# Grouped instance norm in units of 32 channels instead of 16: two 4 MB halves per unit, statistics summed in PSUM

## The chip, the cores and the metric

The kernel runs on one core of a Trainium2 chip. The metric is device time in microseconds (us), one figure per execution; lower is better. The profile is one execution taken by the hardware profiler, with times in us from the start of its span.

With one core there is no second die to compare, so a run is called slow only when it is more than 1.5% above the fastest run of the same kernel.

## The reference

The input is a float32 tensor of 4 x 8 x 16 x 256 x 256, which is 512 channels of 65536 elements, 134 MB. Each channel is normalized by its own mean and variance and scaled by a factor:

```python
mu = x.mean(axis=(3, 4), keepdims=True)
var = ((x - mu) ** 2).mean(axis=(3, 4), keepdims=True)
out = (x - mu) / np.sqrt(var + 1e-5) * gamma[None, :, :, None, None]
```

134 MB must be read and 134 MB written. The arithmetic per element is small.

## The kernel before

A unit is 16 channels. Each channel lies on 8 partitions, so a unit is one tile of 128 partitions x 8192 float32, 4 MB, contiguous in memory. There are 32 units and six tile buffers. SyncE issues the loads, ScalarE the stores. A load into a buffer waits for the store that last used it.

```python
S = 8; K = P // S; F = HW // S; U = n_ch // K      # 16 channels, 8192 columns, 32 units
data = tc.tile_pool(name="data", bufs=6)
for u in range(6): load(u)                         # nc.sync.dma_start, 4 MB each
...
for u in range(U):
    # statistics: one VectorE sum, two ScalarE squares with accumulated sums
    nc.vector.reduce_sum(out=sums[:, 0:1], in_=t[:], axis=AX.X)
    for c in range(0, F, 4096):
        nc.scalar.activation(out=junk[:], in_=t[:, c:c+4096], func=Square, accum_out=sqs[:, n:n+1])
    # ... matmul with a block matrix sums the 8 partitions of a channel;
    # ... eight small VectorE operations and one Sqrt make scale and shift
    # normalization, split: 5376 columns on VectorE, 2816 on ScalarE
    nc.vector.tensor_scalar(out=t[:, :5376], in0=t[:, :5376], scalar1=scale, scalar2=shift, ...)
    nc.scalar.activation(out=t[:, 5376:], in_=t[:, 5376:], func=Identity, bias=shift, scale=scale)
    nc.scalar.dma_start(out=ov[u], in_=t[:])       # the store, 4 MB
    if u + 6 < U: load(u + 6)
```

## Time and profile before

The median was 628.86 us of three runs (628.77 to 629.19) when the prediction was made.

| What | Value | Where it is read |
|---|---|---|
| DMA engines busy | 0.9 or more in all slices but the first and last | the page, slices |
| Bytes moved | 427 to 435 GB/s in most slices | the page, slices |
| VectorE, ScalarE busy | 66%, 54% of the span | the page, part 1 |
| Waits for loads | VectorE 150.4 us, ScalarE 163.5 us | the waits |

These lines are from the page of the kernel before. The lines DMA and GB/s cut the span into 40 slices; each digit is the busy share of the 16 DMA engines in tenths. The queue lines give packets, megabytes and share of all 16 DMA engines (q1 is loads, q10 stores). The line that starts with L109 is a group of instructions, the sums: shapes and count, then busy time and the mean ns of one, then the idle time ahead of them and what ended it. The last two are transfers, with the median time from issue to landing at the end.

```profile
span 627.1 us, 937 instructions
...
PE 22.3 (4%) x80; PEld 19.5 (3%) x80; DVE 416.5 (66%) x324; ACT 336.9 (54%) x194; POOL 1.2 (0%) x7
...
DMA  8999999999999999999999999999999999999997
GB/s 368 435 403 433 435 435 435 433 435 435 435 433 435 435 435 431 433 428 433 435 427 435 431 435 433 433 433 435 435 433 435 435 435 435 433 433 435 435 433 314
...
q1 hardware_dynamic: 4608, 134.22, 49.9%
q10 hardware_dynamic: 4610, 134.22, 49.6%
...
DVE 67%; another core or an unknown queue 23%; PE 3%; DMA 2%; ACT 2%; issue 1%
...
L109 DVE TENSOR_REDUCE sums<-xt 128x1 f32<-128x8192 f32 x32 | 277.9, 8686 | 150.4 <-DMA xt<-in_x_dram 150.4
...
xt<-in_x_dram SPq DMA_DIRECT2D x32, 4096.0 KB, 60.4
out_dram<-xt ACTq DMA_DIRECT2D x32, 4096.0 KB, 41.3
```

The waits of the kernel before, in us in total, count and longest:

```profile
ACT junk L111 <- DMA xt<-in_x_dram: 163.5, 29, 10.4
DVE sums L109 <- DMA xt<-in_x_dram: 150.4, 29, 6.5
```

The DMA engines are full from end to end: 49.9% of their time goes to loads and 49.6% to stores. VectorE and ScalarE wait for loads. The chain names VectorE for 67%, but it walks back along whatever came last; the waits show that the reductions themselves wait for data.

The columns of the timeline are start, duration, engine, line, operation.

```profile
24.30 3.08 DVE L147 TENSOR_SCALAR xt<-xt,scale,shift 128x5376 f32<-128x5376 f32 x1
24.36 2.73 ACT L153 ACTIVATE xt<-xt,shift,scale 128x2816 f32<-128x2816 f32 x1 [0.68 <-DVE shift L143]
...
27.46 0.38 ACTq L168 DMA_DIRECT2D out_dram<-xt  x1
```

```profile
598.43 8.69 DVE L109 TENSOR_REDUCE sums<-xt 128x1 f32<-128x8192 f32 x1 [5.13 <-DMA xt<-in_x_dram]
...
612.76 0.34 ACTq L168 DMA_DIRECT2D out_dram<-xt  x1
```

The first store is issued at 27.46 us, when VectorE has ended its part of the normalization. The last reduction starts at 598.43 us, when the last tile has landed.

### The profile page before, as it was taken

To read this page: it belongs to the slowest core of one execution; us is meant where nothing else is said; L and a number is where in the kernel's file an instruction comes from. 1 tells how busy PE (TensorE), PEld (TensorE's weight loads), DVE (VectorE), ACT (ScalarE), POOL (GpSimd) and SP (SyncE) were. 2 spreads that over 40 slices of the span, in tenths; PEclk is the share of its full clock that TensorE was granted. 3 is DMA by queue.
4 is the path that set the end of the run, shared out by engine and by line. 5 is a ranking of instruction groups with operands and counts; after the bars stand their busy time and mean duration, and the time that the engine had idled before them with its cause. 6 is when DMAs were issued, how large, how long until landed. Compare 5 with 4: busy or idle time off the path is not lost.

```text
span 627.1 us, 937 instructions
## 1 busy us (share of the span) xinstructions
PE 22.3 (4%) x80; PEld 19.5 (3%) x80; DVE 416.5 (66%) x324; ACT 336.9 (54%) x194; POOL 1.2 (0%) x7
## 2 busy tenths in 40 slices
PE   2000000000000000000000000000000000000000
PEld 2000000000000000000000000000000000000000
DVE  2999657766577665686656866558665577655770
ACT  2877536555456464464634646446554455544560
POOL 0000000000000000000000000000000000000000
DMA  8999999999999999999999999999999999999997
GB/s 368 435 403 433 435 435 435 433 435 435 435 433 435 435 435 431 433 428 433 435 427 435 431 435 433 433 433 435 435 433 435 435 435 435 433 433 435 435 433 314
DMA packets 9224, 268.49 MB, mean 428 GB/s; under 512 B 1025, under 2 KB 1026, under 8 KB 1026
## 3 DMA queue, kind: packets, MB, share of 16 engines
q1 hardware_dynamic: 4608, 134.22, 49.9%
q10 hardware_dynamic: 4610, 134.22, 49.6%
q14 instruction: 6, 0.05, 0.0%
HBM read 134.22 MB, written 134.22 MB: 428 GB/s over the span
## 4 chain that ended last, share of the span: by engine, by line
DVE 67%; another core or an unknown queue 23%; PE 3%; DMA 2%; ACT 2%; issue 1%
DVE sums L109 44%; DVE xt L147 16%; PE ps L120 3%; DMA xt<-in_x_dram 2%; ACT std L136 2%; DVE var L131 1%; DVE rstd L138 1%; DVE cm L125 1%; DVE shift L143 1%; DVE scale L141 1%; DVE nmean L127 1%; DVE mv L117 1%; DVE mv L118 0%
## 5 line engine op out<-in xcount | busy, mean ns | idle before, releaser
L109 DVE TENSOR_REDUCE sums<-xt 128x1 f32<-128x8192 f32 x32 | 277.9, 8686 | 150.4 <-DMA xt<-in_x_dram 150.4
L111 ACT ACTIVATE junk<-xt 128x4096 bf16<-128x4096 f32 x64 | 231.5, 3617 | 166.8 <-DMA xt<-in_x_dram 163.5
L147 DVE TENSOR_SCALAR xt<-xt,scale,shift 128x5376 f32<-128x5376 f32 x32 | 98.5, 3079 | 1.2
L153 ACT ACTIVATE xt<-xt,shift,scale 128x2816 f32<-128x2816 f32 x32 | 87.5, 2734 | 22.0 <-DVE shift L143 22.0
L136 ACT ACTIVATE std<-var,eps_t 128x1 f32<-128x1 f32 x32 | 9.4, 294 | 85.4 <-DVE var L131 85.4
L120 PE MATMUL ps<-mv,avg 128*128 128x2 f32 x64 | 18.7, 362 | 582.9 <-DVE mv L118 582.9
L120 PEld LDWEIGHTS ps<-mv,avg 128*128 128x128 f32 x64 | 16.0, 311 | 585.6 <-DVE mv L118 569.8
L125 DVE COPY cm<-ps 128x2 f32<-128x2 f32 x32 | 5.1, 160 | 21.8 <-PE ps L120 21.8
L138 DVE RECIPROCAL rstd<-std 128x1 f32<-128x1 f32 x32 | 5.2, 164 | 11.6 <-ACT std L136 11.6
L111 ACT ACTIVATION_READ_ACCUMULATOR junk<-xt 128x1 f32 x64 | 11.9, 186 | 0.0
L131 DVE SCALAR_TENSOR_TENSOR var<-cm,nmean 128x1 f32<-128x1 f32 x32 | 7.0, 220 | 1.1
L143 DVE TENSOR_TENSOR shift<-nmean,scale 128x1 f32<-128x1 f32 x32 | 5.1, 159 | 1.1
L141 DVE TENSOR_TENSOR scale<-rstd,g_col 128x1 f32<-128x1 f32 x32 | 5.1, 159 | 1.1
L117 DVE TENSOR_REDUCE mv<-sums 128x1 f32<-128x1 f32 x32 | 4.9, 154 | 1.1
L127 DVE TENSOR_SCALAR nmean<-cm 128x1 f32<-128x1 f32 x32 | 4.9, 153 | 1.1
L118 DVE TENSOR_REDUCE mv<-sqs 128x1 f32<-128x2 f32 x32 | 4.7, 145 | 0.0
L92 PE MATMUL g_ps<-one,g_rep 1*128 1x1 f32 x16 | 3.6, 348 | 2.8 <-DVE g_rep L86 2.8
L92 PEld LDWEIGHTS g_ps<-one,g_rep 1*128 1x128 f32 x16 | 3.5, 325 | 2.8 <-DVE g_rep L86 2.8
L99 DVE COPY g_col<-g_ps 128x8 f32<-128x8 f32 x1 | 0.2, 167 | 3.7 <-PE g_ps L92 3.7
L111 ACT ACT_TABLE_LOAD x1 | 1.3, 1283 | 1.4 <-PEq L185 1.4
L86 DVE COPY g_rep<-g_row 1x1024 f32<-1x1024 f32 x1 | 0.7, 681 | 1.1 <-DMA g_row<-in_gamma_dram 1.1
L136 ACT ACT_TABLE_LOAD x1 | 1.3, 1283 | 0.0
(9 smaller groups left out, 1.5 us busy)
## 6 DMA issues: line engine op xcount, KB each, us to landing
xt<-in_x_dram SPq DMA_DIRECT2D x32, 4096.0 KB, 60.4
out_dram<-xt ACTq DMA_DIRECT2D x32, 4096.0 KB, 41.3
g_row<-in_gamma_dram ACTq DMA_DIRECT2D x1, 0.5 KB
```

What stands on the lines that cost most here:

```text
L109: nc.vector.reduce_sum(out=sums[:, j : j + 1], in_=t[:, a:b], axis=AX.X)
L111: nc.scalar.activation(out=junk[:], in_=t[:, c : c + SQ], func=ACTF.Square, accum_out=sqs[:, n : n + 1],)
L117: nc.vector.reduce_sum(out=mv[:, 0:1], in_=sums[:], axis=AX.X)
L120: nc.tensor.matmul(out=ps[:], lhsT=avg[:].rearrange("p k s -> p (k s)"), rhs=mv[:], start=True, stop=True,)
L125: nc.vector.tensor_copy(out=cm[:], in_=ps[:])
L131: nc.vector.scalar_tensor_tensor(out=var[:], in0=cm[:, 0:1], scalar=nmean[:], in1=cm[:, 1:2], op0=ALU.mult, op1=ALU.add,)
L136: nc.scalar.activation(out=std[:], in_=var[:], func=ACTF.Sqrt, bias=eps_t[:], scale=1.0)
L138: nc.vector.reciprocal(out=rstd[:], in_=std[:])
L141: nc.vector.tensor_mul(out=scale[:], in0=rstd[:], in1=g_col[:, g : g + 1])
L143: nc.vector.tensor_mul(out=shift[:], in0=nmean[:], in1=scale[:])
L147: nc.vector.tensor_scalar(out=t[:, a:b], in0=t[:, a:b], scalar1=scale[:], scalar2=shift[:], op0=ALU.mult, op1=ALU.add,)
L153: nc.scalar.activation(out=t[:, a:b], in_=t[:, a:b], func=ACTF.Identity, bias=shift[:], scale=scale[:],)
```

## The change

The intent is fewer instructions. A unit becomes 32 channels on 4 partitions each, 128 partitions x 16384 float32, moved as two 4 MB halves. The partial sums of both halves are accumulated in PSUM by two matmuls, so that one short chain of small operations serves 32 channels. The square of a half is one instruction that writes bytes. The first half is normalized by VectorE alone and the second by ScalarE alone.

```diff
-    S = 8
+    S = 4
+    CW = F // 2
+    AHEAD = 3
-    data = ctx.enter_context(tc.tile_pool(name="data", bufs=6))
+    data = ctx.enter_context(tc.tile_pool(name="data", bufs=2 * AHEAD))
     def load(u):
+        for h in range(2):
+            t = data.tile([P, CW], F32, name="xt")
+            nc.sync.dma_start(out=t[:], in_=xv[u, :, h * CW : (h + 1) * CW])
+            tiles[u, h] = t
...
+        for h in range(2):
+            t = tiles[u, h]
+            nc.vector.reduce_sum(out=st[:, 2 * h : 2 * h + 1], in_=t[:], axis=AX.X)
+            nc.scalar.activation(out=junk[:], in_=t[:], func=ACTF.Square,
+                                 accum_out=st[:, 2 * h + 1 : 2 * h + 2])     # junk is uint8
+            nc.tensor.matmul(out=ps[:], lhsT=navg_w, rhs=st[:, 2 * h : 2 * h + 2],
+                             start=h == 0, stop=h == 1)
...                                       # nvar from PSUM, Sqrt, reciprocal, scale, shift
-            norm_vector(t, 0, DV, scale, shift)
-            norm_scalar(t, DV, F, scale, shift)
-            nc.scalar.dma_start(out=ov[u], in_=t[:])
-        if u + 6 < U:
-            load(u + 6)
+        nc.vector.tensor_scalar(out=ta[:], in0=ta[:], scalar1=scale, scalar2=shift, ...)
+        nc.scalar.activation(out=tb[:], in_=tb[:], func=ACTF.Identity, bias=shift, scale=scale)
+        nc.scalar.dma_start(out=ov[u, :, 0:CW], in_=ta[:])
+        nc.scalar.dma_start(out=ov[u, :, CW:F], in_=tb[:])
+        if u + AHEAD < U:
+            load(u + AHEAD)
```

In memory, a half is now 128 rows of 32 KB at a pitch of 64 KB. Before, a tile was 128 rows of 32 KB that followed each other.

More of the change, by code (lines that the diff above doesn't have):

```diff
@@ L27 @@
     n_ch = B * G * C
-    S = 8
+    S = 4
     K = P // S
     F = HW // S
+    CW = F // 2
     U = n_ch // K
     NG = (G * C) // K
-    SQ = 4096
-    DV = 5376
-    assert HW % S == 0 and (G * C) % K == 0 and F % SQ == 0
+    AHEAD = 3
+    assert HW % S == 0 and (G * C) % K == 0
     xv = x.rearrange("b g c h w -> (b g c h w)").rearrange("(u p f) -> u p f", p=P, f=F)
@@ L45 @@
     ctx.enter_context(tc.manual_schedule())
-    def spans(widths):
-        edges = [0]
-        for w in widths:
-            edges.append(edges[-1] + w)
-        assert edges[-1] == F
-        return list(zip(edges[:-1], edges[1:]))
-    load_spans, store_spans = {}, {}
-    whole = spans([F])
     tiles = {}
     def load(u):
-        t = data.tile([P, F], F32, name="xt")
-        for a, b in load_spans.get(u, whole):
-            nc.sync.dma_start(out=t[:, a:b], in_=xv[u, :, a:b])
-        tiles[u] = t
-    for u in range(6):
+        for h in range(2):
+            t = data.tile([P, CW], F32, name="xt")
+            nc.sync.dma_start(out=t[:], in_=xv[u, :, h * CW : (h + 1) * CW])
+            tiles[u, h] = t
+    for u in range(AHEAD):
         load(u)
@@ L71 @@
     eps_t = singles.tile([P, 1], F32, name="eps_t")
-    nc.vector.memset(eps_t[:], 1e-5)
-    avg = singles.tile([P, K, S], F32, name="avg")
-    nc.gpsimd.memset(avg[:], 1.0 / HW)
+    nc.gpsimd.memset(eps_t[:], 1e-5)
+    one = singles.tile([1, 1], F32, name="one")
+    nc.gpsimd.memset(one[:], 1.0)
+    navg = singles.tile([P, K, S], F32, name="navg")
+    nc.gpsimd.memset(navg[:], -1.0 / HW)
     nc.gpsimd.affine_select(
-        out=avg[:], in_=avg[:], pattern=[[-S, K], [0, S]], compare_op=ALU.is_ge,
+        out=navg[:], in_=navg[:], pattern=[[-S, K], [0, S]], compare_op=ALU.is_ge,
         fill=0.0, base=0, channel_multiplier=1,
@@ L79 @@
     nc.gpsimd.affine_select(
-        out=avg[:], in_=avg[:], pattern=[[S, K], [0, S]], compare_op=ALU.is_ge,
+        out=navg[:], in_=navg[:], pattern=[[S, K], [0, S]], compare_op=ALU.is_ge,
         fill=0.0, base=S - 1, channel_multiplier=-1,
     )
-    one = singles.tile([1, 1], F32, name="one")
-    nc.vector.memset(one[:], 1.0)
+    navg_w = navg[:].rearrange("p k s -> p (k s)")
     g_rep = singles.tile([1, NG, K, S], F32, name="g_rep")
@@ L99 @@
     nc.vector.tensor_copy(out=g_col[:], in_=g_ps[:])
-    junk = singles.tile([P, SQ], BF16, name="junk")
-    def coefficients(u):
-        t = tiles[u]
-        sums = stats_pool.tile([P, len(load_spans.get(u, whole))], F32, name="sums")
-        sqs = stats_pool.tile([P, F // SQ], F32, name="sqs")
-        n = 0
-        for j, (a, b) in enumerate(load_spans.get(u, whole)):
-            nc.vector.reduce_sum(out=sums[:, j : j + 1], in_=t[:, a:b], axis=AX.X)
-            for c in range(a, b, SQ):
-                nc.scalar.activation(
-                    out=junk[:], in_=t[:, c : c + SQ], func=ACTF.Square,
-                    accum_out=sqs[:, n : n + 1],
-                )
-                n += 1
-        mv = stats_pool.tile([P, 2], F32, name="mv")
-        nc.vector.reduce_sum(out=mv[:, 0:1], in_=sums[:], axis=AX.X)
-        nc.vector.reduce_sum(out=mv[:, 1:2], in_=sqs[:], axis=AX.X)
-        ps = psum.tile([P, 2], F32, name="ps")
-        nc.tensor.matmul(
-            out=ps[:], lhsT=avg[:].rearrange("p k s -> p (k s)"), rhs=mv[:],
-            start=True, stop=True,
-        )
-        cm = stats_pool.tile([P, 2], F32, name="cm")
-        nc.vector.tensor_copy(out=cm[:], in_=ps[:])
-        nmean = stats_pool.tile([P, 1], F32, name="nmean")
-        nc.vector.tensor_scalar(
-            out=nmean[:], in0=cm[:, 0:1], scalar1=-1.0, scalar2=None, op0=ALU.mult,
-        )
-        var = stats_pool.tile([P, 1], F32, name="var")
-        nc.vector.scalar_tensor_tensor(
-            out=var[:], in0=cm[:, 0:1], scalar=nmean[:], in1=cm[:, 1:2],
@@ new lines @@
+    junk = singles.tile([P, CW], mybir.dt.uint8, name="junk")
+    for u in range(U):
+        st = stats_pool.tile([P, 4], F32, name="st")
+        ps = psum.tile([P, 2], F32, name="ps")
+        for h in range(2):
+            t = tiles[u, h]
+            nc.vector.reduce_sum(out=st[:, 2 * h : 2 * h + 1], in_=t[:], axis=AX.X)
+            nc.scalar.activation(
+                out=junk[:], in_=t[:], func=ACTF.Square,
+                accum_out=st[:, 2 * h + 1 : 2 * h + 2],
+            )
+            nc.tensor.matmul(
+                out=ps[:], lhsT=navg_w, rhs=st[:, 2 * h : 2 * h + 2],
+                start=h == 0, stop=h == 1,
+            )
+        nmean = ps[:, 0:1]
+        nvar = stats_pool.tile([P, 1], F32, name="nvar")
+        nc.vector.tensor_scalar(
+            out=nvar[:], in0=nmean, scalar1=nmean, scalar2=ps[:, 1:2],
@@ L135, in coefficients @@
         std = stats_pool.tile([P, 1], F32, name="std")
-        nc.scalar.activation(out=std[:], in_=var[:], func=ACTF.Sqrt, bias=eps_t[:], scale=1.0)
-        rstd = stats_pool.tile([P, 1], F32, name="rstd")
-        nc.vector.reciprocal(out=rstd[:], in_=std[:])
-        scale = stats_pool.tile([P, 1], F32, name="scale")
-        g = u % NG
-        nc.vector.tensor_mul(out=scale[:], in0=rstd[:], in1=g_col[:, g : g + 1])
-        shift = stats_pool.tile([P, 1], F32, name="shift")
-        nc.vector.tensor_mul(out=shift[:], in0=nmean[:], in1=scale[:])
@@ L144, in coefficients @@
-        return scale, shift
-    def norm_vector(t, a, b, scale, shift):
+        nc.scalar.activation(out=std[:], in_=nvar[:], func=ACTF.Sqrt, bias=eps_t[:], scale=-1.0)
+        coef = stats_pool.tile([P, 2], F32, name="coef")
+        scale, shift = coef[:, 0:1], coef[:, 1:2]
+        nc.vector.reciprocal(out=std[:], in_=std[:])
+        nc.vector.tensor_mul(out=scale, in0=g_col[:, u % NG : u % NG + 1], in1=std[:])
+        nc.vector.tensor_mul(out=shift, in0=nmean, in1=scale)
+        ta, tb = tiles.pop((u, 0)), tiles.pop((u, 1))
@@ L147, in norm_vector @@
         nc.vector.tensor_scalar(
-            out=t[:, a:b], in0=t[:, a:b], scalar1=scale[:], scalar2=shift[:],
-            op0=ALU.mult, op1=ALU.add,
-        )
-    def norm_scalar(t, a, b, scale, shift):
-        nc.scalar.activation(
-            out=t[:, a:b], in_=t[:, a:b], func=ACTF.Identity, bias=shift[:], scale=scale[:],
-        )
-    for u in range(U):
-        scale, shift = coefficients(u)
-        t = tiles.pop(u)
-        if u in store_spans:
-            for j, (a, b) in enumerate(store_spans[u]):
-                (norm_scalar if j == 1 else norm_vector)(t, a, b, scale, shift)
-            for a, b in store_spans[u]:
-                nc.scalar.dma_start(out=ov[u, :, a:b], in_=t[:, a:b])
-        else:
-            norm_vector(t, 0, DV, scale, shift)
-            norm_scalar(t, DV, F, scale, shift)
-            nc.scalar.dma_start(out=ov[u], in_=t[:])
-        if u + 6 < U:
-            load(u + 6)
+            out=ta[:], in0=ta[:], scalar1=scale, scalar2=shift, op0=ALU.mult, op1=ALU.add,
+        )
```

## The prediction

> **What bounds the kernel now.** The DMA engines. In the page's slices their busy share is nine tenths or more in all but the first and last of 40 slices, at 403 to 435 GB/s; the queue table puts 49.9% of the 16 engines' span in loads, 49.6% in stores. 268.4 MB at 434 GB/s is 618 us of the 627.1 us span. The rest is the start (131 GB/s in the first 2 us, by the windows view), a dip to 386 GB/s from 29 to 39 us when stores begin, and the end (bytes stop near 624 us). Compute waits: VectorE is busy 66%, ScalarE 54%, and the waits view shows VectorE 150 us and ScalarE 164 us waiting for loads. A tile needs 14.3 us from start of its reduction to store issue (598.43 to 612.76, timeline); one tile comes every 19.35 us. The chain of waits names VectorE for 67%; I read that as the path followed back, not the bound: it has 23% of unexplained waits just where reductions wait for loads. The Trainium skill, page "DMA: Bandwidth & Descriptors", section "Specifications", gives 435 GB/s as the fabric ceiling; the trace agrees.
>
> **What the change does.** Same bytes, same 32 KB runs, 64 transfers of 4 MB, six buffers. It removes most small VectorE operations (0.15 to 0.22 us each): VectorE goes from 324 instructions to about 100, from 416 us busy to 16 x (2 x 8.69 + about 4.55 + 0.8) = about 365. ScalarE: square of 8192 about 7.0 us, normalization of 8192 about 7.2 us (from 3617 ns at 4096 and 2733 ns at 2816, with the slope of 0.83 ns an element in the Trainium skill, page "ScalarE: Activation LUTs", section "What ACT_TABLE_LOAD costs", which fits both); 16 x (14.4 + 7.2 + 0.3) = about 350 us. None of it lies on the DMA's path.
>
> **What it moves.** The unit's granularity. First store about 40 us instead of 27.5 (second half lands near 22.7, then 8.7 reduce + 1.7 coefficients + 7.2 normalization). Until then the six prefetched loads, 58 us of work, keep DMA busy. In steady state 8 MB come every 38.7 us and hold their buffers about 18 us after the second half landed; of six buffers 4.6 are on average with DMA, so a queue is never empty. Loads should land in about 38 us (now 60), stores in 40 and 60 us (now 41). The last load lands near 585 us (now 598), because more stores are still queued; its two stores are issued near 603 us, while earlier stores drain, so no bubble: bytes again stop near 624 us.
>
> **Predicted: 628.6 us, 80% range 626.0 to 633.0.** Faster by over 2%: 0.02; within 2%: 0.94; slower by over 2%: 0.04.
>
> **What would show it.** Slices at 430 to 435 GB/s; VectorE about 58% busy, ScalarE about 56%; last load near 585 us; last store issue near 603 us with DMA share still 1.0; span 626 to 628 us.
>
> **What would make it wrong.** (1) The row pitch in memory doubles from 32 to 64 KB within a transfer; should that slow reads or writes, every slice shows it (under 425 GB/s). (2) A bubble at the end: if earlier stores finish before 603 us, up to some 8 us are lost. (3) Queue sharing other than half and half, so that loads starve and a slice falls below nine tenths. (4) A better end or start could gain 1 to 3 us; nothing can gain 2%.

## The result and the profile after

The changed kernel took 663.96 us (median of 6 runs, 655.82 to 667.54), against 628.97 us for the kernel before. The ratio is 1.05, with a 95% interval of 1.044 to 1.056. All ratios here are the mean time of one kernel's fast runs over that of the other's in the same rounds, so they are not quite the ratio of the medians. The changed kernel's six times were 664.59, 666.21, 663.33, 658.45, 655.82 and 667.54: they spread by 1.8%, where the kernel before spreads by 0.2%.

The same lines of its page (the sums are now L99, and L124 is VectorE's normalization of a first half):

```profile
span 662.9 us, 619 instructions
...
PE 19.8 (3%) x72; PEld 17.8 (3%) x72; DVE 363.4 (55%) x114; ACT 350.6 (53%) x98; POOL 1.5 (0%) x9
...
DMA  9999999999999999999999999999999999999447
GB/s 380 441 413 423 427 433 413 429 423 421 429 416 435 415 429 419 418 415 441 421 425 427 427 419 401 423 390 409 413 405 433 395 397 427 399 423 418 198 206 320
...
q1 hardware_dynamic: 4608, 134.22, 48.3%
q10 hardware_dynamic: 4610, 134.22, 48.2%
...
DMA 69%; another core or an unknown queue 12%; DVE 11%; ACT 3%; PE 1%; issue 0%; SPq 0%; ACTq 0%
...
L99 DVE TENSOR_REDUCE st<-xt 128x1 f32<-128x8192 f32 x32 | 277.8, 8685 | 250.1 <-DMA xt<-in_x_dram 250.1
...
L124 DVE TENSOR_SCALAR xt<-xt,coef 128x8192 f32<-128x8192 f32 x16 | 72.7, 4546 | 0.6
...
xt<-in_x_dram SPq DMA_DIRECT2D x32, 4096.0 KB, 41.0
out_dram<-xt ACTq DMA_DIRECT2D x32, 4096.0 KB, 46.3
```

And the same two waits:

```profile
DVE st L99 <- DMA xt<-in_x_dram: 250.1, 29, 13.4
ACT junk L100 <- DMA xt<-in_x_dram: 237.8, 29, 15.0
```

The instruction part came out as computed: VectorE is busy 363.4 us (416.5 before) and ScalarE 350.6 us. Two other things are new. In the middle of the run the DMA engines are as busy as before, at 0.9 or more, but move only 390 to 441 GB/s. At the end there are two slices at four tenths.

The end, first by its timeline, then in windows (busy time of each engine, then the clock, the DMA share and GB/s):

```profile
584.23 0.33 SPq L52 DMA_DIRECT2D xt<-in_x_dram  x1
...
623.20 8.69 DVE L99 TENSOR_REDUCE st<-xt 128x1 f32<-128x8192 f32 x1 [10.67 <-DMA xt<-in_x_dram]
...
638.44 0.34 ACTq L128 DMA_DIRECT2D out_dram<-xt  x1
641.16 0.34 ACTq L129 DMA_DIRECT2D out_dram<-xt  x1
```

```profile
core 0: us, PE busy (x) PEld busy (x) DVE busy (x) ACT busy (x) POOL busy (x), PEclk, DMA share, GB/s
609.00:615.00 6.00, 0.56 (x2) 0.50 (x2) 3.52 (x1) 2.02 (x2) 0.00 (x0) 1.00 0.99 426
617.60:630.00 12.40, 0.00 (x0) 0.00 (x0) 6.80 (x1) 6.75 (x1) 0.00 (x0) 1.00 0.25 106
630.00:637.00 7.00, 0.56 (x2) 0.50 (x2) 5.79 (x6) 3.76 (x4) 0.00 (x0) 1.00 0.07 28
640.00:652.00 12.00, 0.00 (x0) 0.00 (x0) 0.00 (x0) 1.13 (x1) 0.00 (x0) 1.00 1.02 437
```

From 630 to 637 us the DMA share is 0.07 and 28 GB/s move. One sixteenth is 0.0625, and a single engine moves 32 KB in 1.213 us, which is 27.0 GB/s. So one DMA engine out of 16 was at work. The semaphore writes, explained next, show what held the others up. 15 engines had landed their part of the last load by 601.3 us, the last one only at 623.2 us, and the statistics of the last unit need the whole of it. By 621.8 us the 15 had also ended all earlier stores, so they had nothing left until the last unit's stores were issued, at 638.44 us. The one late engine was still busy with those earlier stores: its part of them ended at 632.9 and 642.5 us.

The trace also has the semaphore write with which every engine ends its part of a transfer, and the duration of each 32 KB packet (one row of a tile). It does not name the engine of a packet. From these I worked out two measures, which the rest uses (no view of the profile prints them):

```
                         32 KB packets   over     time above 1.213 us,   last engine behind the median
                         in all          1.26 us  us per engine          one, at the end of a store
before                   8192            46       2.0                    0.2 to 2.4 us
after                    8192            655      17.7                   rises from 0.3 to 33 us, then 21
```

In the kernel before nearly every packet takes 1.213 us. In the changed one 8% take longer, up to 2.9 us, which is 15.7 us more for an engine on average (17.7 - 2.0). Loads and stores keep 48.3% and 48.2% of the engines' time, in a longer span and for the same bytes. One engine also falls behind the others by about 1 to 2 us with each store, up to 33 us at the 20th of 32 stores; then the others can't run ahead any more, because the buffers are not freed. At the two stores before the last two it is 21 us behind. By the queue shares an engine is on average idle for 23 us of the span in place of 3 (3.5% of 662.9, 0.5% of 627.1), nearly all of it the wait at the end. 15.7 us of longer packets and 20 us of idle time make up the 35.8 us by which the span grew (662.9 - 627.1).

### The profile page after: what moved, and what is told of

Read it like the earlier page. It is cut to its first block, busy times and chain, and to the rows that moved or that the text cites. A ratio compares the mean times of both kernels' runs of the same rounds, so it can differ in the third digit from the quotient of the medians.

```text
span 662.9 us, 619 instructions
## 1 busy us (share of the span) xinstructions
PE 19.8 (3%) x72; PEld 17.8 (3%) x72; DVE 363.4 (55%) x114; ACT 350.6 (53%) x98; POOL 1.5 (0%) x9
## 3 DMA queue, kind: packets, MB, share of 16 engines
q1 hardware_dynamic: 4608, 134.22, 48.3%
q10 hardware_dynamic: 4610, 134.22, 48.2%
## 4 chain that ended last, share of the span: by engine, by line
DMA 69%; another core or an unknown queue 12%; DVE 11%; ACT 3%; PE 1%; issue 0%; SPq 0%; ACTq 0%
DMA out_dram<-xt 35%; DMA xt<-in_x_dram 34%; DVE st L99 8%; DVE xt L124 3%; ACT xt L127 2%; PE ps L104 1%; SPq L52 0%; ACT std L116 0%; DVE nvar L111 0%; ACT L116 0%; DVE std L119 0%; DVE coef L120 0%; DVE coef L121 0%; ACTq L127 0%
## 5 line engine op out<-in xcount | busy, mean ns | idle before, releaser
L99 DVE TENSOR_REDUCE st<-xt 128x1 f32<-128x8192 f32 x32 | 277.8, 8685 | 250.1 <-DMA xt<-in_x_dram 250.1
L100 ACT ACTIVATE junk<-xt 128x8192 uint8<-128x8192 f32 x32 | 224.9, 7030 | 238.7 <-DMA xt<-in_x_dram 237.8
L127 ACT ACTIVATE xt<-xt,coef 128x8192 f32<-128x8192 f32 x16 | 115.4, 7214 | 10.9 <-DVE coef L121 10.9
L124 DVE TENSOR_SCALAR xt<-xt,coef 128x8192 f32<-128x8192 f32 x16 | 72.7, 4546 | 0.6
L104 PE MATMUL ps<-st,navg 128*128 128x2 f32 x64 | 17.9, 350 | 610.1 <-DVE st L99 569.9
L104 PEld LDWEIGHTS ps<-st,navg 128*128 128x128 f32 x64 | 16.0, 311 | 612.0 <-issue 571.5
L116 ACT ACTIVATE std<-nvar,eps_t 128x1 f32<-128x1 f32 x16 | 4.7, 294 | 37.0 <-DVE nvar L111 37.0
L111 DVE TENSOR_SCALAR nvar<-ps 128x1 f32<-128x1 f32 x16 | 4.6, 288 | 12.1 <-PE ps L104 12.1
L119 DVE RECIPROCAL std<-std 128x1 f32<-128x1 f32 x16 | 2.6, 164 | 7.1 <-ACT std L116 7.1
L100 ACT ACTIVATION_READ_ACCUMULATOR junk<-xt 128x1 f32 x32 | 6.0, 186 | 0.0
## 6 DMA issues: line engine op xcount, KB each, us to landing
out_dram<-xt ACTq DMA_DIRECT2D x32, 4096.0 KB, 46.3
```

What stands on the lines that cost most here:

```text
L99: nc.vector.reduce_sum(out=st[:, 2 * h : 2 * h + 1], in_=t[:], axis=AX.X)
L100: nc.scalar.activation(out=junk[:], in_=t[:], func=ACTF.Square, accum_out=st[:, 2 * h + 1 : 2 * h + 2],)
L104: nc.tensor.matmul(out=ps[:], lhsT=navg_w, rhs=st[:, 2 * h : 2 * h + 2], start=h == 0, stop=h == 1,)
L111: nc.vector.tensor_scalar(out=nvar[:], in0=nmean, scalar1=nmean, scalar2=ps[:, 1:2], op0=ALU.mult, op1=ALU.add,)
L116: nc.scalar.activation(out=std[:], in_=nvar[:], func=ACTF.Sqrt, bias=eps_t[:], scale=-1.0)
L119: nc.vector.reciprocal(out=std[:], in_=std[:])
```

## The experiments

The order below is the order in which they ran. The first twelve led to the cause, and six more separated its two parts and fixed its limits.

### Addresses or rhythm: e1 and e2

The first two theories were these. The doubled row pitch could slow the packets. Or the rhythm could: stores in pairs, buffers freed in pairs. The two can be swapped. e1 gives the old program the new addresses; e2 gives the new program the old ones. Their outputs are wrong, which doesn't matter for the times.

```diff
 # e1, on the kernel before: half(v, u) = v[u // 2, :, (u % 2) * F : (u % 2 + 1) * F], v with rows of 2 * F
-            nc.sync.dma_start(out=t[:, a:b], in_=xv[u, :, a:b])
+            nc.sync.dma_start(out=t[:, a:b], in_=half(xw, u)[:, a:b])
-            nc.scalar.dma_start(out=ov[u], in_=t[:])
+            nc.scalar.dma_start(out=half(ow, u), in_=t[:])
 # e2, on the changed kernel: xv, ov with f = F // 2
-            nc.sync.dma_start(out=t[:], in_=xv[u, :, h * CW : (h + 1) * CW])
+            nc.sync.dma_start(out=t[:], in_=xv[2 * u + h])
-        nc.scalar.dma_start(out=ov[u, :, 0:CW], in_=ta[:])
-        nc.scalar.dma_start(out=ov[u, :, CW:F], in_=tb[:])
+        nc.scalar.dma_start(out=ov[2 * u], in_=ta[:])
+        nc.scalar.dma_start(out=ov[2 * u + 1], in_=tb[:])
```

> The kernel before, with its instructions and their order unchanged, but each 4 MB load and store goes to the addresses of the changed kernel (rows of 32 KB at a pitch of 64 KB). The result is wrong on purpose. Address theory (the pitch slows packets and makes one DMA engine fall behind): 655 to 668 us, packets of 1.3 to 2 us, one engine some 15 to 30 us behind the others at the end. Rhythm theory (pairs of stores and three loads that land later empty a queue now and then, and each restart and the wait for the slowest engine cost time): 627 to 631 us, as before.

> The changed kernel, with its instructions and their order unchanged, but each 4 MB load and store is one contiguous block, as before. The result is wrong on purpose. Address theory: 627 to 632 us, no engine left behind at the end. Rhythm theory: 655 to 668 us, with DMA share near a sixteenth for some 15 us before the last stores. If both matter, both runs lie between.

e1 took 629.12 us (ratio 1.0001). e2 took 667.24, 667.84, 643.30 and 650.40 us (ratio of its fast runs 1.028). The pitch is not the cause. The Trainium skill, page "DMA: Bandwidth & Descriptors", section "Latency and other measured facts", reports that row pitches of large powers of two slow copies between HBM tensors, 512 KiB slightly and 2 MiB and more strongly; at the 64 KB e1 shows no loss.

### Pairs or depth: e3, e4 and e5

So it is something in the program. e3 makes the old program work in pairs. e4 takes one buffer from it. e5 takes the pairs out of the new program.

```diff
 # e3, on the kernel before
-    for u in range(U):
-        scale, shift = coefficients(u)
-        t = tiles.pop(u)
+    for u0 in range(0, U, 2):
+        pair = [(u, *coefficients(u)) for u in (u0, u0 + 1)]
+        for u, scale, shift in pair:
+            t = tiles.pop(u)
             ...                              # normalization and store as before
+        for u, _, _ in pair:
+            if u + 6 < U: load(u + 6)
 # e4, on the kernel before: bufs=6 -> bufs=5, and load(u + 6) -> load(u + 5)
 # e5, on the changed kernel: after the square of half 0 of unit u,
+            if h == 0 and held:
+                finish(*held)   # second half of unit u - 1: Identity, store, load of its next tile
```

> The kernel before, all its instructions and addresses kept, but two units at a time: statistics of both, then the normalization and store of both, so two stores are issued 3 us apart every 38.7 us and six buffers are freed in pairs. Rhythm theory (pairs): 640 to 668 us, one or two DMA engines some 15 to 30 us behind at the end. Instruction theory (what matters is the changed instructions: the unsplit normalization of a whole half by one engine, the square written as bytes, the coefficients read from PSUM): 627 to 631 us.

> The kernel before with five buffers in place of six and nothing else changed. With 0.74 buffers in compute on average, 4.26 are with DMA, fewer than in the changed kernel (about 4.6). Depth theory (too few transfers in flight): slower than 640 us. Pair theory (only the bunching matters): 627 to 632 us.

> The changed kernel, but the second half of a unit is normalized and stored after the square of the next unit's first half, so stores are issued and buffers freed one by one, some 17 to 20 us apart; the result is right. It holds one buffer some 16 us longer, so 4.2 buffers are with DMA on average. Pair theory: 627 to 634 us and all engines end together. Depth theory: as slow as the changed kernel or slower (655 us or more). Instruction theory: as the changed kernel.

e3 took 629.97 us (1.0019), e4 628.86 us (0.9999) and e5 663.23 us (1.056). My rhythm theory fell: pairs in the old program cost next to nothing, and the new program without pairs is as slow as with them. Depth fell as well, since five buffers are enough in the old program.

### Which instruction: e6 to e9

What was left were the changed instructions. I moved the square and the normalization one at a time, in both directions.

```diff
 # e6, on the kernel before: SQ = 4096 -> 8192, junk bf16 -> uint8
 # e7, on the kernel before
-            norm_vector(t, 0, DV, scale, shift)
-            norm_scalar(t, DV, F, scale, shift)
+            (norm_scalar if u % 2 else norm_vector)(t, 0, F, scale, shift)
 # e8, on the changed kernel: two squares of 4096 into bf16, and nc.vector.reduce_sum of the two sums
 # e9, on the changed kernel, for each half t
+            nc.vector.tensor_scalar(out=t[:, :5376], in0=t[:, :5376], ...)
+            nc.scalar.activation(out=t[:, 5376:], in_=t[:, 5376:], func=ACTF.Identity, ...)
+            nc.scalar.dma_start(out=ov[u, :, h * CW : (h + 1) * CW], in_=t[:])
```

> The kernel before with only the square changed to the changed kernel's: one 8192-wide ScalarE instruction per tile that writes bytes, in place of two 4096-wide ones that write bf16. If the square is the instruction that matters: 640 to 668 us with DMA engines falling behind. If the normalization or the statistics' layout is: 628 to 631 us. Neither explains yet how an instruction slows a DMA engine.

> The kernel before with only the normalization changed: even units by VectorE alone, odd units by ScalarE alone, each 8192 wide. If the unsplit normalization matters: 640 to 668 us. If the square or the layout does: 628 to 631 us.

> The changed kernel with only the square changed back: two 4096-wide ScalarE instructions per half that write bf16, and one small VectorE sum. If the square matters: 628 to 633 us. Otherwise 655 to 668 us.

> The changed kernel with only the normalization changed back: each half split 5376 for VectorE and 2816 for ScalarE, so the first store is issued earlier than the second and neither engine is long at it. If the unsplit normalization matters: 628 to 633 us. Otherwise 655 to 668 us.

e6 took 629.23 us (1.0012) and e7 630.06 us (1.0024), so neither instruction hurts the old program. e8 took 656.30, 667.27, 643.72 and 650.26 us (fast runs 1.029). e9 took 627.98 us (0.9987): splitting the normalization again removes the whole loss. Yet e7 does not split it and is fast. An instruction that hurts in one program and not in the other is not the cause by itself; it may change something else.

What it changes is when the first store is issued. The changed kernel's unsplit VectorE normalization takes 4.55 us, so its first store comes at 39.24 us:

```profile
34.66 4.55 DVE L124 TENSOR_SCALAR xt<-xt,coef 128x8192 f32<-128x8192 f32 x1
34.72 7.21 ACT L127 ACTIVATE xt<-xt,coef 128x8192 f32<-128x8192 f32 x1 [0.68 <-DVE coef L121]
...
39.24 0.38 ACTq L128 DMA_DIRECT2D out_dram<-xt  x1
41.96 0.34 ACTq L129 DMA_DIRECT2D out_dram<-xt  x1
```

In e9 it comes at 37.70 us. Until the first store only loads run, at 9.7 us a tile or 1.2 us a row of 32 KB on each engine. From then on each engine takes mostly one row of the load and one of the store in turn. The Trainium skill, page "DMA: Bandwidth & Descriptors", section "Queues, rings and completion order", says that an engine goes round its queues packet by packet; the trace agrees, with a change of queue after most 32 KB records (where the times leave only one engine for a record to follow on, in 3173 of 3581 cases in the kernel before). In such a rotation the offset between the store's row and the load's row, set at the first store, is kept: in the kernel before it stays the same for 29 stores. I call it the position: the end of a store tile minus the end of the nearest load tile, both from the semaphore writes. One row is 2.4 us of it, a load row and a store row. In the changed kernel it holds at about +2.4 us for the first ten stores only; from then on the late engine holds up the buffers, and the position of the others wanders.

All runs up to here, sorted in that way: the position of most engines, how many engines are one row off from it, and the median of all times. The counts are read from the 16 ends of the first store and of the load beside it, in the one execution that was profiled. The positions of e2 and e8 come from executions labelled slow.

```
run     first store issued, us   position of most engines   engines one row off   time, us
e1      27.14                    -2.4                       none                  629.1
e6      27.38                    -2.4                       none                  629.2
before  27.46                    -2.4                       none                  629.0
e4      27.47                    -2.4                       none                  628.9
e9      37.70                    0 (about 9 engines)        7, at -2.4            628.0
e3      38.47                    0                          1, at +2.4            630.0
e7      28.91                    0                          none                  630.1
e5      39.14                    +2.4                       1, at 0               663.2
e8      39.17                    +2.4                       4, at 0               653.3
after   39.24                    +2.4                       1, at 0               664.0
e2      39.41                    +2.4                       2, at 0               658.8
```

Every slow run has its stores one row behind its loads. In each, a few engines took the first store a row earlier relative to their loads. The semaphore writes don't name the engine, but the number that then falls behind is the same: one in the changed kernel and in e5, two in e2, four in e8.

### The moment of the first store alone: e10, e11 and e12

This theory makes a prediction that no instruction theory makes. A delay of the first store alone, in one unit out of 32, must make the old kernel slow; an earlier first store alone must make the changed kernel fast.

```diff
 # e10, on the kernel before, ahead of the store of unit 0 only
+            if u == 0:
+                nc.scalar.activation(out=t[:, F - 2720 :], in_=t[:, F - 2720 :], func=ACTF.Identity)
 # e11, on the changed kernel: the split normalization of e9 for unit 0 only, units 1 to 15 as changed
 # e12, on the changed kernel, after VectorE's normalization of unit 0 only
+        if u == 0:
+            nc.vector.tensor_scalar(out=ta[:, :1792], in0=ta[:, :1792], scalar1=1.0, ...)
```

> The kernel before, with one extra ScalarE copy of about 2.45 us ahead of its very first store, which is then issued near 29.6 us and not at 27.46; the other 31 units are untouched, the result is right. Phase theory (what matters is at which row of a running load the store stream starts: in the slow runs every engine's stores end their tile one row, 2.4 us, after its loads, in the fast runs 2.4 us before them or together): the phase becomes +2.4 us as in the slow runs, one engine or more falls behind, 640 to 668 us. Instruction theory (the unsplit normalization of every unit in a kernel of halves is to blame): 629 to 632 us.

> The changed kernel, with the normalization of its first unit alone split over both engines, so that the first store is issued near 37.7 us and not at 39.24; the other 15 units keep the unsplit normalization, the result is right. Phase theory: phase about -0.3 us, 627 to 631 us. Instruction theory: 652 to 667 us, since 15 of 16 units are as in the changed kernel.

> The changed kernel, with one extra VectorE instruction of about 1.2 us on the first unit's first half, so that its first store is issued near 40.5 us and not at 39.24. Phase theory: the phase moves on by a row, to +4.8 us, and the time may change either way; if only the phase of +2.4 us is bad, 627 to 633 us; if every store that trails its load is, 645 us or more. Instruction theory: 655 to 668 us, as the changed kernel.

e10 took 669.45, 651.75, 672.05 and 668.55 us. Its fastest run is 3.6% above the 628.91 us of the kernel before in those rounds. One copy of some 2.5 us in a kernel of 629 us cost 23 to 43 us. Its first store and the slices of its page (this profile is from an execution labelled slow):

```profile
29.74 0.38 ACTq L171 DMA_DIRECT2D out_dram<-xt  x1
```

```profile
DMA  9999999999999999999999999999999999896556
GB/s 377 436 412 430 424 416 418 434 416 422 422 414 434 412 432 422 422 424 412 434 405 432 418 422 423 422 420 422 426 416 432 430 432 420 330 413 279 220 247 261
```

Both signs of the changed kernel are there: lower GB/s at full DMA busy share, then a starved end.

e11 took 627.88 us (0.9984), with 15 of its 16 units exactly as in the changed kernel:

```profile
37.76 0.38 ACTq L135 DMA_DIRECT2D out_dram<-xt  x1
```

```profile
DMA  8999999999999999999999999999999999999998
GB/s 369 435 402 435 435 433 427 433 435 435 435 432 433 429 435 435 430 431 435 435 433 429 433 433 435 433 431 435 429 435 435 431 431 435 435 434 425 433 435 352
```

The two signs are gone. As far as the ends tell, half of the engines of e11 were at 0 and half at -2.4 us, and being a row apart did no harm there. e12 took 630.25, 643.62, 642.04 and 632.93 us (fast runs 1.0043). In it 14 engines were at +4.8 us and two at +2.4. Two of its four times lie above the 627 to 633 us that were expected if +2.4 us alone is bad. The two engines at +2.4 may be why, but the profile is of the fastest execution and doesn't show it.

### The split or the position: e13, e14 and e15

In the changed kernel and in e10 two things come together, the position of +2.4 us and the few engines that are a row off (two in e10, and two fall behind). I call an edge a moment of the first store at which some engines still take it a row earlier than the rest. e13 and e14 put the first store between two edges, so that engines agree. e15 changes the distance in memory between the tile that is loaded and the one that is stored.

```diff
 # e13: as e12, 650 columns in place of 1792
 # e14: as e10, 3200 columns in place of 2720
 # e15, on the changed kernel: order = [5 * u % U for u in range(U)], used for load, gamma and store
```

> The changed kernel with an extra VectorE instruction of about 0.5 us on the first unit's first half: first store near 39.75 us, between the edge at about 39.2 and the one at about 40.3. All 16 engines should then end their stores 2.4 us after their loads. Edge theory: 627 to 632 us. Position theory: 645 to 668 us.

> The kernel before with the extra ScalarE copy of the first unit lengthened by 0.4 us over the earlier delay run: first store near 30.15 us in place of 29.74. All 16 engines at +2.4 us. Edge theory: 628 to 633 us, so that 0.4 us more delay takes back 20 to 40 us. Position theory: 645 to 672 us, as with the shorter delay.

> The changed kernel with the same timing, but units are loaded, computed and stored in the order 0, 5, 10, 15, 4, ... so the tile being loaded and the tile being stored lie 80 or 48 MB apart and not 16 MB; the result is right. If the distance of the two streams in memory matters for the engines that fall behind: another time, possibly 627 to 635 us. If not: 655 to 668 us.

e13 took 641.82 us (1.022, interval 1.0183 to 1.0255, so unclear by the limit of 2%), first store at 39.62 us, all 16 engines at +2.4. e14 took 644.50 us (1.024, interval 1.0222 to 1.0256), first store at 30.43 us, 15 engines at +2.4 and one further behind. The slices of e13:

```profile
DMA  9999999999999999999999999999999999999997
GB/s 390 427 398 427 437 433 429 433 420 427 420 425 427 418 433 427 409 431 420 427 427 418 429 412 433 429 414 427 416 437 427 410 435 402 429 431 419 429 422 304
```

The starved end is gone, the lower rate is not. Both times lie between what the two theories expected. So both readings hold, each for a part. The position alone costs some 13 us in the changed kernel and some 16 us in the old one (641.82 - 628.97, 644.50 - 628.97). The engines that are a row off cost the rest of the changed kernel's loss, some 20 us: 22 us between the medians (663.96 - 641.82), 18 us between the means of the fast runs (660.5 - 642.7). That also fits that 0.7 us more delay made the old kernel faster, from e10 to e14. The packets differ too: of the time above 1.213 us per engine, loads have 12.1 of 12.8 us in e13, but 9.2 of 17.7 in the changed kernel, where stores are stretched as well.

e15 took 664.36, 653.68, 659.31 and 663.32 us (fast runs 1.047), like the changed kernel. The distance between the two tiles in memory did not matter there. It was not changed for the position alone, as in e13.

### How wide the bad range is: e16, e17 and e18

```diff
 # e16, e17: as e12, 2950 and 5260 columns in place of 1792
 # e18: as e10, 4485 columns in place of 2720
```

> The changed kernel, extra VectorE instruction of the first unit lengthened so that the first store is issued near 40.95 us: all engines at +4.8 us. If only +2.4 us is bad: 627 to 631 us. If every store stream that trails its load stream is: 640 us or more.

> The same, with the first store near 42.15 us: all engines at +7.2 us. If only +2.4 us is bad: 627 to 632 us. If every trailing position is: 640 us or more.

> The kernel before, extra ScalarE copy of the first unit lengthened so that the first store is issued near 31.5 us: all engines at +4.8 us. If only +2.4 us is bad: 628 to 632 us, faster than with the shorter delays. If every trailing position is: 640 us or more.

e16 took 627.37 us (0.9977), e17 627.28 us (0.9974, interval 0.9959 to 0.9989) and e18 628.66 us (0.9997). Lines of e16:

```profile
41.16 0.38 ACTq L132 DMA_DIRECT2D out_dram<-xt  x1
42.15 0.34 ACTq L133 DMA_DIRECT2D out_dram<-xt  x1
```

```profile
DMA  8999999999999999999999999999999999999998
GB/s 369 436 402 436 436 436 436 436 436 436 434 428 423 429 432 436 434 436 436 436 436 434 434 434 434 427 430 427 436 434 436 436 434 436 434 436 434 434 429 352
```

A first store that comes 1.9 us later than the changed kernel's (41.16 against 39.24 us) makes it 36.6 us faster. e17 is the fastest kernel, 0.26% below the kernel before. The counts of slow packets agree (e12's are of the execution that took 630.25 us):

```
run      first store, us   position        packets over 1.26 us   us per engine above 1.213   time, us
e10      29.74             +2.4, two at 0  794                    15.5                        669.0
e13      39.62             +2.4            653                    12.8                        641.8
e14      30.43             +2.4, one more  640                        14.0                        644.5
e12      40.33             +4.8, two +2.4  101                        2.3                         637.5
e16      41.16             +4.8            115                    1.8                         627.4
e18      31.56             +4.8, three +7.2 47                        1.8                         628.7
e17      42.03             +7.2            48                         1.5                         627.3
```

Measured positions of -2.4, 0, +4.8 and +7.2 us are harmless to within 0.3%, apart from e12 with its two engines at +2.4. A position of +2.4 us costs 2.2% (e13) and 2.4% (e14), and more with engines a row off.

### What stays open

Why the position of one row behind stretches packets is not settled. In e13 the packets of two engines can be followed from end to end, as far as their times tell engines apart, and 10.7 of 11.4 us and 8.2 of 9.1 us of their stretched load time lie in the first three rows of a load tile, where the store stream is at its last row or at the first rows of its next tile. Those are the rows at which both transfers change over. That the change-over is the cause is only a reading of where the time lies; no run took it away, and none changed where the two tiles lie on the chip. Why an engine one row off falls behind the others is open in the same way. Other row sizes were not tried either.

## Why the prediction was wrong

- What bounds the kernel: right. DMA is busy at 0.9 or more in the middle of every run here, and e4 and e6 changed buffers and instructions without effect.
- The cost of instructions: right. VectorE was predicted at 365 us and measured at 363.4, ScalarE at 350 and measured at 350.6. In the middle of the run none of it was on the DMA's path, as predicted. At the start it set the moment of the first store, and at the end the last unit's 15 us (623.20 to 638.44) passed with only one DMA engine at work.
- The first store at about 40 us: measured 39.24. The figure was right and its meaning was missed. I took the moment to be harmless because the six loads keep DMA busy, and 1.9 us more (e16) or 1.5 us less (e9) of it is worth 36 us.
- "In steady state ... a queue is never empty", loads in 38 us and stores in 40 and 60: measured medians were 41.0 and 46.3 us. Queues did run empty late in the run, for 15 engines that waited for one.
- "The last load lands near 585 us", "its two stores are issued near 603 us", "so no bubble": wrong. The last load's reduction starts at 623.20, the last store is issued at 641.16, and ahead of it the DMA share is 0.07.
- The step that failed is that bytes again stop near 624 us with the rate unchanged. It treated the 16 DMA engines as one pipe with a fixed rate, shared between two queues. The runs showed that the rate depends on how the two streams lie against each other (some 13 us at one row behind), and that 16 engines with separate queues need not stay together (some 20 us).
- Of the listed risks, (1) the row pitch was tested and cleared by e1, and (3) unequal sharing was not what happened. (2) named a bubble at the end, of up to 8 us, if earlier stores finish before the last are issued. On 15 engines they did, at 621.8 us against 638.44, but the reason was not foreseen: one engine's part of the last load landed 22 us after the others' (623.2 against 601.3). The range of 626 to 633 us had no room for a loss of that kind.

## What to carry to other kernels

When a kernel runs at the limit of the DMA engines, a change off the critical path can still move it by 5%, by shifting when the store stream starts against the load stream; so before blaming the edited instructions, shift the first store alone by a row or two and see whether the time follows. Look at the DMA share and the GB/s together: here full share with fewer bytes meant stretched packets, and a share near one sixteenth meant that one engine was late. A spread of 1 to 4% between executions of one kernel, where its neighbour spreads by 0.2%, was here a sign of a start on an edge; its absence was no proof, since e5, with one engine a row off, spread by only 0.8%.

## What the Trainium skill lacked or had wrong

- "DMA: Bandwidth & Descriptors", "Queues, rings and completion order", describes rotation between queues but not that the offset between two long streams is fixed at the start and kept while the engines stay together, nor that it matters: 627.4 us at two rows behind, 641.8 us at one row behind, with the same program but for the length of one instruction (e16, e13).
- The same section expects a queue to be drained for about 9 to 17 descriptors before an engine changes; here the engines changed queue after most single 32 KB records while more rows of the same tile were queued. The trace does not say how many descriptors a record is.
- The same page, "Why a DMA increments its semaphore by 16 and not by 1", says that engines finish independently; it gives no size. Here one engine ended a store up to 33 us after the median engine (changed kernel), against at most 2.4 us in the kernel before.
- The same page, "Specifications", gives about 27 GiB/s per engine; a 32 KB row in 1.213 us is 27.0 GB/s (25.2 GiB/s).
